# Making four expert-table blocks ready in empty buffers beside the query projection, and starting the gathers one step later, in a hybrid encoder layer on Trainium2

## The chip, the cores and the metric

The kernel runs on one core of a Trainium2 chip. The metric is device time in microseconds (us) of one execution; the time of a kernel is the median of its runs. Engines are named as the profile names them: PE is TensorE (the matmuls), PEld its weight load, DVE is VectorE, ACT is ScalarE, POOL is GpSimd, SP is SyncE, which here only issues DMA transfers.

## The reference

One layer: two parallel head groups, cross-attention into 256 memory tokens, and an expert-retrieval feed-forward part (PEER). The change touches the last one alone. `D_MODEL` is 1024, the sequence has 512 tokens, there are 8 retrieval heads, 128 x 128 = 16384 experts of one neuron each, and each head keeps 16 experts for a token.

```python
def _peer(h, w_query, sub_keys, expert_u, expert_v):
    B, S, D = h.shape
    q = (h @ w_query).reshape(B, S, PEER_HEADS, 2, PEER_KEY_DIM)
    sc = jnp.einsum('bshpk,hpnk->bshpn', q, sub_keys).astype(jnp.float32)
    v1, i1 = lax.top_k(sc[..., 0, :], PEER_TOPK)
    v2, i2 = lax.top_k(sc[..., 1, :], PEER_TOPK)
    n_cand = PEER_TOPK * PEER_TOPK
    cand = (v1[..., :, None] + v2[..., None, :]).reshape(B, S, PEER_HEADS, n_cand)
    cand_idx = (i1[..., :, None] * N_KEYS + i2[..., None, :]).reshape(B, S, PEER_HEADS, n_cand)
    top_s, pos = lax.top_k(cand, PEER_TOPK)
    idx = jnp.take_along_axis(cand_idx, pos, axis=-1)
    g = jax.nn.softmax(top_s, axis=-1).astype(h.dtype)
    ...
    def block(args):
        xt, it, gt = args
        u = expert_u[it]
        act = jax.nn.gelu(jnp.einsum('td,tkd->tk', xt, u))
        return jnp.einsum('tk,tkd->td', gt * act, expert_v[it])
```

## The kernel before, in words

Every fp32 matmul is made of three on fp32r halves (`mm3`, L109): a weight tile is split into a high half `wh` (a cast on ACT) and a low half `wl` (the rest).

The 512 tokens are four tiles of 128. For tile 0 the selected rows of both expert tables are gathered, one row per token and slot: 128 gathers from U and 128 from V, in order, by indirect DMA from POOL, each followed by one DVE instruction (`gather_step`, L1101). For tiles 1 to 3 (384 tokens) the kernel computes all 16384 experts densely: for each of 128 blocks e of 128 experts, `mm1(e)` multiplies U block e by the tokens (24 matmuls of 384 columns) and applies GeLU; the result lies in a buffer `act` until `weigh(e)` multiplies it by the gate weights, and `second` multiplies it by V block e. `mm1` runs `LAG` = 40 blocks ahead of `second`; the pool `acts` has 42 buffers of 128 x 384.

Stages, in the order of the program:

- Query projection (L853 to L905): for n = 0 to 15 a block `pq` of the query weight is multiplied (`proj`), the query is copied (`query`), scored against its keys (`key_scores`), and DVE takes the first 16 of each head half (`first_level`).
- Blocks ahead of the rows (L1033 to L1039): while `second_level(1)` selects the 16 experts of each head for token tile 1 on DVE, PE computes the first `U_MID` = 10 blocks of U. The generator `second_level` yields after each of its 15 steps.
- One-hot rows (L1041 to L1085): for tiles 1 to 3 the gate weights are scattered into a dense matrix `Wd` in DRAM: 32 groups of four tokens a tile, each with `hot` and `wei` on DVE and eight matmuls (L1063), an eviction on ACT, and a store for every four groups. Between groups parts of further `mm1` blocks are emitted at a `rate` that reaches block 37 at the end, and steps of `second_level` for the next tile.
- Main loop (L1204 to L1256), in an order written by hand: three more blocks, then 128 steps e, each with `mm1(e + 40)`, `weigh`, two steps of `second_level(0)` twice, gathers up to `due(e + 0.4)` and `due(e + 1)`, and `second`. `due` gives no gather before step `G_AT`, and spreads 215.6 of the 256 up to step 88 whatever `G_AT` is. For tile 0 the temporary tiles of `second_level` lie in the gather buffers (`Rooms`).

Outside the hand-ordered part a scheduler orders each engine's instructions by program order and readiness; each engine then runs them strictly in that order.

Weights come through `Weights`: `plan` lists all blocks in order of use, `get` hands out the next, `fill` loads and casts up to `DEPTH` = 2 ahead, `fill_low` makes the low halves. The pool `wp` has three buffers each of `w`, `wh` and `wl`. For most blocks U0 to U36 the low half is made by a DMA: ACT writes -w into `wl` (L144) and POOL issues a transfer that adds w minus the rounding (L145); blocks 11, 14, ..., 35 and 37 to 39 are split by DVE (L174). A raw buffer `w` is free again when its low half is done.

Of the kernel before, what the change touches and what calls it, by code (L numbers as in the profile page):

```python
# [10 lines left out]
F32 = mybir.dt.float32  # L11
F32R = mybir.dt.float32r
# [4 lines left out]
AF = mybir.ActivationFunctionType  # L17
# [12 lines left out]
ND = DT * 128  # L30
NE = 128
LAG = 40
U_MID = 10
SPARE = 3
WGB = 3
GPB = 4
# [11 lines left out]
OFF1 = 600  # L48
OFF2 = 10
LEVEL = 2, 3  # L50
G_AT = 3
L_MID = 2
WARM = 9
QAHEAD = 1
# [22 lines left out]
def layer(ctx, tc, a, out, upto=99, dbg=None):  # L77
    nc = tc.nc
    dbg = dbg or {}
    V, A, PE, SP, PL = nc.vector, nc.scalar, nc.tensor, nc.sync, nc.gpsimd  # L80

    def pool(stack, name, bufs=1, **kw):
        return stack.enter_context(tc.tile_pool(name=name, bufs=bufs, **kw))
# [9 lines left out]
    def bank(name="bk"):  # L93
        return psum.tile([128, 512], F32, name=name, tag="bk")
# [5 lines left out]
    def split(hi, lo, src):  # L100

        A.copy(hi, src)
        V.tensor_sub(lo, src, hi.bitcast(F32))
# [5 lines left out]
    def mm3(ps, terms, first=True, last=True):  # L109
        n = len(terms)  # L110
        for c, (lh, ll, rh, rl) in enumerate(terms):
            PE.matmul(ps, lh, rh, start=first and c == 0, stop=False)  # L112
            PE.matmul(ps, lh, rl, start=False, stop=False)  # L113
            PE.matmul(ps, ll, rh, start=False, stop=last and c == n - 1)  # L114

    class Weights:

        def __init__(self, plan):  # L120
            self.plan, self.raw, self.ready, self.at, self.low, self.used = plan, {}, {}, 0, 0, 0
            self.more = None

        def low_tile(self, key, shape):

# [1 line left out]
            return pool.tile(shape, F32R, name="wl")  # L127

        def fill(self, n, cuts=(slice(None),), between=None):
            while self.at < min(n, len(self.plan)):  # L130
                key = self.plan[self.at]
                self.at += 1
                src, shape, by_dma = source(*key)
                w = wp.tile(shape, F32, name="w")
                wh = wp.tile(shape, F32R, name="wh")
                for cs in cuts:
                    SP.dma_start(w[:, cs], src[:, cs])
                    A.copy(wh[:, cs], w[:, cs])  # L138
                    if between:
                        between.pop()()  # L140
                wl = None
                if by_dma:
                    wl = self.low_tile(key, shape)
                    A.activation(wl, w, AF.Copy, scale=-1.0)  # L144
                    PL.dma_start(wl, w, accum_op=OP.add)  # L145
                self.raw[key] = w, wh, wl, shape
# [17 lines left out]
            self.at = self.low = n  # L164

        def fill_low(self, n, cuts=(slice(None),)):
            while self.low < min(n, len(self.plan)):
                key = self.plan[self.low]
                self.low += 1
                w, wh, wl, shape = self.raw.pop(key)  # L170
                if wl is None:
                    wl = self.low_tile(key, shape)
                    for cs in cuts:
                        V.tensor_sub(wl[:, cs], w[:, cs], wh[:, cs].bitcast(F32))  # L174
                self.ready[key] = wh, wl

        def get(self, *key, ahead=DEPTH):
            assert self.plan[self.used] == key, (self.plan[self.used], key)
            self.used += 1
            self.fill(self.used + ahead)  # L180
            self.fill_low(self.used + min(1, ahead))
            return self.ready.pop(key)

    def source(kind, n):
        one = [128, NCH, 128]
        if kind == "v":
            return a["w_v"][:, 2 * n:2 * n + 2], [128, 2, 512], kind in BY_DMA
        if kind == "mv":
            return a["w_vm"][:, n], [128, D], kind in BY_DMA
        if kind == "U":  # L190
            return a["U"][n], [128, D], n < LAG - U_DMA and n not in U_V
        if kind == "V":
            return a["V"][n * 128:(n + 1) * 128], [128, D], False
        at = {"xl": ("w_in", 0), "gt": ("w_in", 4), "q": ("w_in", 8), "k": ("w_in", 12), "mk": ("w_km", 0),
              "wo": ("w_out", 0), "qm": ("w_qm", 0), "om": ("w_om", 0), "pq": ("w_pq", 0)}[kind]
        return a[at[0]][at[1] + n], one, kind in BY_DMA
# [14 lines left out]
    W = Weights(plan)  # L211

    def proj(key, ops, n=S, **kw):
        wh, wl = W.get(*key, **kw)
        ps = bank()
        mm3(ps[:, :n], [(wh[:, c], wl[:, c], h[:, :n], l[:, :n]) for c, (h, l) in enumerate(ops)])
        return ps
# [73 lines left out]
    views, at = {}, 0  # L291
# [523 lines left out]
    ap = pool(ctx, "acts", LAG + 2, side="right")  # L815
# [19 lines left out]
    def mm1_next():  # L835
        ahead[0] += 1
        return mm1_parts(ahead[0] - 1)

    top_pool = ExitStack()
    tp = pool(top_pool, "top")  # L840
# [12 lines left out]
    with tc.tile_pool(name="qp", bufs=1) as qp:  # L853
        QS, SC, KEY = {}, {}, {}

        def load_keys(n):
            if n < 16:
                KEY[n] = qp.tile([128, 128], F32, name="kr", bufs=4)
                SP.dma_start(KEY[n], a["keysT"][n])

        def query(n):
            ps = PQ.pop(n)
            QS[n] = qp.tile([128, S], F32, name="q", bufs=3)
            if n < NQ:
                V.tensor_mul(QS[n], ps, R3)
            else:
                A.copy(QS[n], ps)
            load_keys(n + 2)

        def key_scores(n):  # L870

            SC[n] = qp.tile([128, TT, 128], F32, name="sc", bufs=4)
            ps = bank()
            for t in range(TT):
                ts = slice(t * 128, (t + 1) * 128)
                PE.matmul(ps[:, ts], QS[n][:, ts], KEY[n], start=True, stop=True)  # L876
            A.copy(SC[n].rearrange("p t n -> p (t n)"), ps)

        def first_level(n):
            h, p = divmod(n, 2)  # L880
            v, x, sc = [y[:, h, p] for y in vals], [y[:, h, p] for y in idxs], SC[n]
            rest = [qp.tile([128, 128], F32, name="s2", bufs=4) for t in range(TT)]
            for t in range(TT):
                V.max(v[t][:, :8], sc[:, t])
            for t in range(TT):
                V.max_index(x[t][:, :8], v[t][:, :8], sc[:, t])
            for t in range(TT):
                V.match_replace(rest[t], v[t][:, :8], sc[:, t], LOW)
            for t in range(TT):
                V.max(v[t][:, 8:], rest[t])  # L890
            for t in range(TT):
                V.max_index(x[t][:, 8:], v[t][:, 8:], rest[t])

        load_keys(0)
        load_keys(1)
        query(0)
        for n in range(16):
            if NQ <= n + QAHEAD < 16:
                PQ[n + QAHEAD] = proj(("pq", n + QAHEAD), ho)
            if n + 1 < 16:  # L900
                query(n + 1)
            key_scores(n)
            if n:
                first_level(n - 1)
        first_level(15)  # L905


    Wd = dram.tile([128, 8 * DT, NE, 16], F32)
    HK = [128, 8, 16]
# [24 lines left out]
    def second_level(t, tp):  # L934
# [10 lines left out]
        top = tp.tile(HK, F32, name="tops")  # L945
        pos = tp.tile(HK, U32, name="pos")
        for h0 in range(0, 8, 4):
# [13 lines left out]
                V.max_index(pos[:, h, 8:], top[:, h, 8:], c2[:, h - h0])  # L961
            yield

        p7 = tp.tile(HK, U32, name="p7")
        p3 = tp.tile(HK, U32, name="p3")
        ov = tp.tile(HK, F32, name="ov")
# [14 lines left out]
        for p in range(2):  # L981
# [11 lines left out]
            V.tensor_add(dst.rearrange("p (h k) -> p k h", k=16), eq[:, 0], eq[:, 1])  # L993
            out.append(dst)
            yield

        ex = tp.tile(HK, F32, name="ex")
        su = sm.tile([128, 8], F32, name="su8")
        gF = tp.tile([128, 128], F32, name="gF", bufs=2)
        V.tensor_sub(ex, top, top[:, :, 0:1].to_broadcast(HK))  # L1000
        A.activation(ex, ex, AF.Exp)
        V.tensor_reduce(su, ex, axis=AX.X, op=OP.add)
        V.reciprocal(su, su)
        V.tensor_mul(gF.rearrange("p (h k) -> p h k", k=16), ex, su[:, :, None].to_broadcast(HK))
# [19 lines left out]
    def hurried(steps, offset):  # L1024
        while True:
            with tc.high_priority(offset=offset) if offset else ExitStack():
                if next(steps, 0) == 0:
                    return
            yield

    with (tc.tile_pool(name="wg", bufs=2) as wg, tc.tile_pool(name="st", bufs=2, side="right") as stages,
          tc.tile_pool(name="wx", bufs=1) as W.more):
        parts, owed = iter(()), 0.0  # L1033
        done = 0
        for k, _ in enumerate(hurried(second_level(1, tp), OFF1)):
            while ahead[0] < LAG and done < (k + 1) * U_MID / 15 and done < U_MID:
                done += 1
                for _ in mm1_next():
                    pass  # L1039
        rate = (LAG - SPARE - ahead[0]) * NCH / (DT * 32)  # L1040
        for tile_ in range(1, TT):  # L1041
            level = hurried(second_level(tile_ + 1, tp) if tile_ < DT else iter(()), OFF2)
            ij, gg = SEL.pop(tile_)
            for q in range(8):
                tb = (tile_ - 1) * 8 + q
                stage = stages.tile([128, NE, 16], F32, name="stage", tag="stage")
                for t4 in range(0, 16, 4):
# [22 lines left out]
                    while owed >= 1:  # L1070
                        owed -= 1
                        if next(parts, 0) == 0 and ahead[0] < LAG - SPARE:
                            parts = mm1_next()
# [79 lines left out]
    def due(e):  # L1153

        full = NE - LAG
        late = (256 - G_RATE * full) / (LAG - G_END)
        return math.ceil(G_RATE * max(min(e, full) - G_AT, 0) * full / (full - G_AT) + late * max(e - full, 0))

# [46 lines left out]
    order.enter_context(tc.manual_schedule())  # L1205

    level = second_level(0, Rooms(gp))

    def level_steps(n):
# [111 lines left out]
```

## Time and profile before

| | us |
|---|---|
| median of 3 runs (1628.90 to 1629.57) | 1629.24 |
| the profiled execution, its own time | 1627.87 |
| its span, from the first to the last instruction | 1626.1 |
| PE busy | 1592.0 |
| DVE busy | 1267.4 |
| ACT busy | 753.7 |
| POOL busy | 469.4 |

Times in the profile count from the start of the span. A matmul's record is longer than the distance to the next one, since matmuls are pipelined: the distance between starts is what a matmul costs. A record in brackets tells how long the engine stood idle before the instruction and what ended the wait.

### The profile page before, as it was taken

To read this page: it belongs to the slowest core of one execution; us is meant where nothing else is said; L and a number is where in the kernel's file an instruction comes from. 1 tells how busy PE (TensorE), PEld (TensorE's weight loads), DVE (VectorE), ACT (ScalarE), POOL (GpSimd) and SP (SyncE) were. 2 spreads that over 40 slices of the span, in tenths; PEclk is the share of its full clock that TensorE was granted. 3 is DMA by queue.
4 is the path that set the end of the run, shared out by engine and by line. 5 is a ranking of instruction groups with operands and counts; after the bars stand their busy time and mean duration, and the time that the engine had idled before them with its cause. 6 is when DMAs were issued, how large, how long until landed. Compare 5 with 4: busy or idle time off the path is not lost.

```text
span 1626.1 us, 23694 instructions
## 1 busy us (share of the span) xinstructions
PE 1592.0 (98%) x8512; PEld 1401.8 (86%) x8512; DVE 1267.4 (78%) x2525; ACT 753.7 (46%) x1194; POOL 469.4 (29%) x345
## 2 busy tenths in 40 slices
PE   9999999999997999999999999999999999999997
PEld 7788888888887888998999999999999999988886
DVE  7878885555979997887777777777777777788887
ACT  6568753456455676643333333333333333333334
POOL 0111000001111100004455454444444554453331
PEclk9999999999999999999999999999999999999999
DMA  7444452127777899977989889998898898999993
GB/s 257 123 136 146 126 164 96 56 74 222 168 174 174 257 308 269 300 234 276 316 300 320 307 301 320 312 318 308 291 332 313 298 317 309 307 328 335 319 329 145
DMA packets 156359, 405.83 MB, mean 250 GB/s; under 512 B 13793, under 2 KB 63073, under 8 KB 153169
## 3 DMA queue, kind: packets, MB, share of 16 engines
q1 hardware_dynamic: 110736, 242.36, 43.4%
q0 software_dynamic: 45504, 161.96, 32.5%
q8 instruction: 66, 1.08, 0.3%
q14 instruction: 53, 0.43, 0.1%
HBM read 348.69 MB, written 29.36 MB: 232 GB/s over the span
## 4 chain that ended last, share of the span: by engine, by line
PE 87%; DVE 4%; DMA 4%; ACT 2%; issue 2%; POOL 0%; DVEq 0%; SPq 0%; ACTq 0%; POOLq 0%
PE acc L1167 31%; PE bk L112 16%; PE bk L113 15%; PE bk L114 15%; PE bk L1063 2%; DMA w<-in_U 1%; DMA Wd<-stage 1%; PE om L113 1%; PE om L114 1%; PE om L112 1%; PE bk L876 1%; DVE hot L1054 1%; DVE wei L1058 1%; PE pv L112 1%; PE pv L113 1%
## 5 line engine op out<-in xcount | busy, mean ns | idle before, releaser
L138 ACT CAST wh<-w 128x1024 fp32r<-128x1024 f32 x330 | 347.3, 1053 | 339.6 <-PE acc L1167 200.9
L112 PE MATMUL bk<-hH,wh 128*128 128x384 f32 (+1 forms) x1128 | 394.5, 350 | 4.2 <-ACT wh L138 4.2
L114 PE MATMUL bk<-hH,wl 128*128 128x384 f32 (+1 forms) x1128 | 386.8, 343 | 7.9 <-DVE wl L174 3.0
L113 PE MATMUL bk<-hL,wh 128*128 128x384 f32 (+1 forms) x1128 | 385.4, 342 | 0.0
L174 DVE TENSOR_TENSOR wl<-w,wh 128x1024 fp32r<-128x1024 f32 x286 | 348.6, 1219 | 26.8 <-ACT wh L138 26.5
L1097 POOL DMA_INDIRECT g<-in_Un,gidx x128 | 206.0, 1609 | 242.6 <-DVE junk L1104 197.5
L1097 POOL DMA_INDIRECT g<-in_V,gidx x128 | 199.1, 1555 | 229.0 <-DVE gacc L1114 213.0
L1167 PE MATMUL acc<-wh,ph 128*128 128x512 f32 x768 | 238.6, 391 | 0.0
L1167 PE MATMUL acc<-wh,pl 128*128 128x512 f32 x768 | 238.1, 391 | 0.0
L1167 PE MATMUL acc<-wl,ph 128*128 128x512 f32 x768 | 238.1, 390 | 0.0
L114 PEld LDWEIGHTS bk<-hH,wl 128*128 128x128 f32 x1128 | 212.7, 189 | 13.8 <-DMA wl<-w 3.9
L112 PEld LDWEIGHTS bk<-hH,wh 128*128 128x128 f32 x1128 | 213.0, 189 | 11.8 <-ACT wh L138 4.8
L113 PEld LDWEIGHTS bk<-hL,wh 128*128 128x128 f32 x1128 | 213.0, 189 | 7.0
L1144 DVE TENSOR_TENSOR pl<-act,ph 128x384 fp32r<-128x384 f32 x128 | 71.1, 557 | 181.8 <-ACT ph L1141 181.8
L826 ACT ACTIVATE act<-bk 128x384 f32<-128x384 f32 x128 | 62.8, 493 | 282.6 <-PE bk L114 282.5
L145 POOL DMA_DIRECT2D wl<-w x44 | 37.8, 858 | 485.2 <-ACT wl L144 444.1
L1167 PEld LDWEIGHTS acc<-wl,ph 128*128 128x128 f32 x768 | 144.1, 188 | 31.6
L1167 PEld LDWEIGHTS acc<-wh,pl 128*128 128x128 f32 x768 | 144.1, 188 | 31.2
L1167 PEld LDWEIGHTS acc<-wh,ph 128*128 128x128 f32 x768 | 142.9, 188 | 24.2
L1114 DVE SCALAR_TENSOR_TENSOR gacc<-g,gu,gacc 128x1024 f32<-128x1024 f32 x127 | 162.5, 1279 | 0.7
L1104 DVE SCALAR_TENSOR_TENSOR junk<-g,htok 128x1024 bf16<-128x1024 f32 x128 | 156.0, 1219 | 6.0 <-DMA g<-in_Un,gidx 5.1
L112 PE MATMUL bk<-oh,wh 128*128 128x512 f32 x280 | 111.8, 400 | 0.1
(338 smaller groups left out, 2140.8 us busy)
## 6 DMA issues: line engine op xcount, KB each, us to landing
w<-in_U SPq DMA_DIRECT2D x128, 512.0 KB, 5.2
w<-in_V SPq DMA_DIRECT2D x128, 512.0 KB, 5.9
Wd<-stage SPq DMA_DIRECT2D x24, 1024.0 KB, 6.6
wt<-Wd SPq DMA_DIRECT2D x90, 256.0 KB, 6.9
wl<-w POOLq DMA_DIRECT2D x44, 512.0 KB, 6.1
w<-in_w_pq SPq DMA_DIRECT2D x16, 512.0 KB, 4.8
w<-in_w_in SPq DMA_DIRECT2D x14, 512.0 KB, 3.5
x<-in_xT SPq DMA_DIRECT2D x16, 256.0 KB, 4.6
```

The costliest lines, as they stand in the source:

```text
L112: PE.matmul(ps, lh, rh, start=first and c == 0, stop=False)
L113: PE.matmul(ps, lh, rl, start=False, stop=False)
L114: PE.matmul(ps, ll, rh, start=False, stop=last and c == n - 1)
L138: A.copy(wh[:, cs], w[:, cs])
L145: PL.dma_start(wl, w, accum_op=OP.add)
L174: V.tensor_sub(wl[:, cs], w[:, cs], wh[:, cs].bitcast(F32))
L826: A.activation(ACT[e], ps[:, :ND], AF.Gelu_apprx_tanh)
L1097: PL.indirect_dma_start(out=g, out_offset=None, in_=a[table], in_offset=bass.IndirectOffsetOnAxis(ap=gidx[:, k:k + 1], axis=0))
L1104: V.scalar_tensor_tensor(junk, g, 1.0, htok, op0=OP.mult, op1=OP.mult, accum_out=gu[:, st:st + 1])
L1114: V.scalar_tensor_tensor(gacc, g, gu[:, k:k + 1], gacc, op0=OP.mult, op1=OP.add)
L1144: V.tensor_sub(PS[e][1], ACT.pop(e), PS[e][0].bitcast(F32))
L1167: PE.matmul(acc[t, hf], lhs[:, ts], rhs[:, hf * 512:(hf + 1) * 512], start=e == 0 and part == 0, stop=e == NE - 1 and part == 2)
```

## The change

Four things change.

- `U_EARLY`: after steps 7, 9, 11 and 13 of the query projection, `Weights.early` makes one of the blocks U0 to U3 ready. It loads the block in thirds (384, 384 and 256 columns) into buffers of the pool `acts`, and splits each third with a cast on ACT and a subtraction on DVE: nine buffers a block, 36 of the 42. `Thirds` lets the matmuls index the three pieces as one tile.
- `reach` lets `fill` and `fill_low` go as many blocks further as there are early ones among those not yet used, so that the three `wp` buffers go to U4, U5, U6.
- `U_MID` is 8 instead of 10: two blocks more are emitted among the one-hot rows.
- In `second_level` the exponential `ex` stands right after the second selection; before, it stood after the index steps. `G_AT` is 4 instead of 3.

```diff
-U_MID = 10
+U_MID = 8
+U_EARLY = 7, 9, 11, 13
...
-G_AT = 3
+G_AT = 4
...
+    class Thirds:
+        def __init__(self, parts):
+            self.parts = parts
+        def __getitem__(self, at):
+            k, c = divmod(at[1].start, ND)
+            return self.parts[k][:, c:c + at[1].stop - at[1].start]
...
-            self.more = None
+            self.more, self.lead = None, set()
+
+        def reach(self, n, at):
+            return min(n + sum(key in self.lead for key in self.plan[self.used:at]), len(self.plan))
+
+        def early(self, key, pool):
+            src, shape, _ = source(*key)
+            thirds = [slice(k, min(k + ND, shape[1])) for k in range(0, shape[1], ND)]
+            parts = []
+            for cs in thirds:
+                n = cs.stop - cs.start
+                w, wh, wl = [pool.tile([128, ND], dt, name=k, tag="act")[:, :n]
+                             for k, dt in (("ew", F32), ("eh", F32R), ("el", F32R))]
+                SP.dma_start(w, src[:, cs])
+                split(wh, wl, w)
+                parts.append((wh, wl))
+            self.ready[key] = [Thirds([p[k] for p in parts]) for k in range(2)]
+            self.lead.add(key)
...
         def fill(self, n, cuts=(slice(None),), between=None):
-            while self.at < min(n, len(self.plan)):
+            while self.at < self.reach(n, self.at):
                 key = self.plan[self.at]
                 self.at += 1
+                if key in self.ready:
+                    continue
...
         def fill_low(self, n, cuts=(slice(None),)):
-            while self.low < min(n, len(self.plan)):
+            while self.low < self.reach(n, self.low):
                 key = self.plan[self.low]
                 self.low += 1
+                if key in self.ready:
+                    continue
...
         def get(self, *key, ahead=DEPTH):
             self.used += 1
+            self.lead.discard(key)
...
             if n:
                 first_level(n - 1)
+            if n in U_EARLY:
+                W.early(("U", U_EARLY.index(n)), ap)
         first_level(15)
...
                 V.max_index(pos[:, h, 8:], top[:, h, 8:], c2[:, h - h0])
             yield
 
+        ex = tp.tile(HK, F32, name="ex")
+        V.tensor_sub(ex, top, top[:, :, 0:1].to_broadcast(HK))
+        A.activation(ex, ex, AF.Exp)
+
         p7 = tp.tile(HK, U32, name="p7")
...
             yield
-
-        ex = tp.tile(HK, F32, name="ex")
         su = sm.tile([128, 8], F32, name="su8")
         gF = tp.tile([128, 128], F32, name="gF", bufs=2)
-        V.tensor_sub(ex, top, top[:, :, 0:1].to_broadcast(HK))
-        A.activation(ex, ex, AF.Exp)
         V.tensor_reduce(su, ex, axis=AX.X, op=OP.add)
```

## Rows read from the trace of the kernel before

**Rows 1.** From the page, busy time and share of the span of PE and its weight load, with the number of instructions.

```profile
PE 1592.0 (98%) x8512; PEld 1401.8 (86%) x8512; DVE 1267.4 (78%) x2525; ACT 753.7 (46%) x1194; POOL 469.4 (29%) x345
```

**Rows 2.** Busy time by stretches. Columns: the stretch in us, its length, the busy time of each engine in it (with the number of instructions), the granted clock of PE, the share of the DMA engines, GB/s.

```profile
400.00:450.00 50.00, 50.00 (x254) 42.56 (x253) 42.84 (x290) 26.05 (x37) 6.32 (x9) 1.00 0.77 185
...
481.00:535.00 54.00, 44.98 (x245) 43.05 (x243) 51.44 (x266) 28.85 (x39) 7.71 (x9) 0.97 0.74 178
535.00:577.00 42.00, 39.95 (x340) 35.47 (x339) 39.07 (x109) 32.73 (x53) 4.29 (x5) 1.00 0.90 268
...
604.00:650.00 46.00, 45.27 (x388) 40.92 (x388) 37.62 (x55) 30.07 (x50) 4.29 (x5) 1.00 0.90 275
650.00:705.00 55.00, 55.00 (x471) 50.06 (x469) 46.92 (x74) 33.16 (x54) 3.62 (x5) 1.00 0.88 294
...
760.00:1590.00 830.00, 830.00 (x4107) 744.07 (x4107) 644.48 (x812) 292.43 (x404) 394.99 (x249) 1.00 0.91 314
```

**Rows 3.** PE's instructions in order of time, from the first table block to the one-hot rows. Columns: start in us, length, engine, line, operation, tiles and shapes, count, idle time before it and what ended it.

```profile
480.88 0.42 PE L112 MATMUL bk<-hH,wh 128*128 128x384 f32 x1
...
504.18 0.44 PE L114 MATMUL bk<-hH,wl 128*128 128x384 f32 x1 [1.34 <-DMA wl<-w]
...
510.31 0.44 PE L112 MATMUL bk<-hH,wh 128*128 128x384 f32 x1 [1.69 <-ACT wh L138]
...
512.78 0.66 PE L114 MATMUL bk<-hH,wl 128*128 128x384 f32 x1 [1.86 <-DVE tops L951]
...
518.76 0.33 PE L114 MATMUL bk<-hH,wl 128*128 128x384 f32 x1
...
519.28 0.33 PE L114 MATMUL bk<-hH,wl 128*128 128x384 f32 x1
...
524.69 0.44 PE L112 MATMUL bk<-hH,wh 128*128 128x384 f32 x1 [2.47 <-ACT wh L138]
...
528.53 0.44 PE L114 MATMUL bk<-hH,wl 128*128 128x384 f32 x1 [1.65 <-DMA wl<-w]
```

**Rows 4.** The instructions that write PSUM banks from 478 to 545 us, grouped by line; shortest, median and longest in ns, start of the first and of the last.

```profile
L1063 PE MATMUL bk<-wei,hot x48: 218/218/238, 535.1 to 544.6; 128*128 128x128 f16 x48
```

**Rows 5.** The chain of work that ended last, from 470 to 580 us, in order of time: start, length, what. "issue" is time in which the engine waited for nothing that the profile shows.

```profile
494.25 3.97 DMA w<-in_U
...
499.74 8.36 issue
508.11 4.54 DMA wl<-w
512.71 5.96 DMA w<-in_U
```

**Rows 6.** Instructions of ACT and of POOL in order of time, same columns as rows 3.

```profile
503.95 0.78 ACT L984 CAST kn<-idx 128x128 f16<-128x128 uint32 x1 [3.65 <-DVE idx L892]
...
506.75 1.07 ACT L144 ACTIVATE wl<-w 128x1024 fp32r<-128x1024 f32 x1 [1.17 <-DVE idx L892]
...
481.65 0.86 POOL L145 DMA_DIRECT2D wl<-w  x1 [5.49 <-ACT wl L144]
```

**Rows 7.** Steps 2 to 4 of the main loop: PE's instructions, then DVE's, same columns.

```profile
743.29 0.45 PE L114 MATMUL bk<-hH,wl 128*128 128x384 f32 x1 [0.75 <-DVE wl L174]
...
754.09 0.45 PE L114 MATMUL bk<-hH,wl 128*128 128x384 f32 x1 [2.25 <-DVE wl L174]
...
755.07 0.51 PE L113 MATMUL bk<-hL,wh 128*128 128x384 f32 x1
...
758.26 0.45 PE L114 MATMUL bk<-hH,wl 128*128 128x384 f32 x1
...
740.65 0.29 DVE L1002 TENSOR_REDUCE su<-g 128x8 f32<-128x128 f32 x1 [2.00 <-ACT g L1001]
...
748.73 1.23 DVE L1104 SCALAR_TENSOR_TENSOR junk<-g,htok 128x1024 bf16<-128x1024 f32 x1 [3.42 <-DMA g<-in_Un,gidx]
```

**Rows 8.** DVE's instructions in order of time: the end of the selection for tile 1, for tile 2, and the wait after it.

```profile
508.63 0.37 DVE L993 TENSOR_TENSOR sel<-eq 128x128 f32<-128x128 f16 x1
...
533.45 0.38 DVE L993 TENSOR_TENSOR sel<-eq 128x128 f32<-128x128 f16 x1
...
535.76 0.69 DVE L1054 TENSOR_TENSOR hot<-io,ij 128x1024 f16<-128x1024 f16 x1 [1.59 <-PE bk L1063]
```

**Rows 9.** Waits of PE over the whole span: who waited for whom, us in total, times, the longest.

```profile
PE bk L1063 <- DVE wei L1058: 2.7, 5, 0.7
```

**Rows 10.** Beside the query projection: issues of SP's queue, then instructions of ACT; the last line is a cast of 128 x 384 from the main loop.

```profile
378.90 2.18 SPq L859 DMA_DIRECT2D kr<-in_keysT  x4
...
399.79 1.07 ACT L809 COPY xt<-bk 128x512 f32<-128x512 f32 x2 [2.78 <-DMA x3d<-xt]
...
433.95 1.04 ACT L138 CAST wh<-w 128x1024 fp32r<-128x1024 f32 x1 [3.37 <-issue]
...
717.72 0.50 ACT L1141 CAST ph<-act 128x384 fp32r<-128x384 f32 x1
```

**Rows 11.** From the page: a group of instructions (busy us in total, mean ns of one | idle time before), and two of the DMA issues (KB each, median us from issue to landing).

```profile
L1144 DVE TENSOR_TENSOR pl<-act,ph 128x384 fp32r<-128x384 f32 x128 | 71.1, 557 | 181.8 <-ACT ph L1141 181.8
...
w<-in_U SPq DMA_DIRECT2D x128, 512.0 KB, 5.2
...
x<-in_xT SPq DMA_DIRECT2D x16, 256.0 KB, 4.6
```

## Prediction

> **What bounds the kernel now.** I read the page first. TensorE (PE) is busy 98% of the span [rows 1], so only the stretches in which PE stands still or runs slowly can be won. The list of busy time by stretches comes second: PE has no loss from 400 to 450 us nor from 760 to 1590, and loses 9 of the 54 us from 481 to 535 and 2 of 42 after that [rows 2]. For these places, and for the start of the main loop, I then read PE's instructions in order of time with the idle time before each, the chain of waits, and the same stretch of ScalarE (ACT), VectorE (DVE) and GpSimd (POOL).
>
> First place: the ten table blocks ahead of the one-hot rows. Their first matmul starts at 480.9 [rows 3] and the first one-hot matmul at 535.1 [rows 4]: 54.2 us. Three matmuls start every 0.52 us (518.76 to 519.28), so a block of 24 takes 4.16 us and ten take 41.6; 12.6 us are lost. Five waits make 9.0 of them (1.34 + 1.69 + 1.86 + 2.47 + 1.65) [rows 3]; the rest is slower matmuls and short gaps. The chain says why: a raw block is loaded (3.97 us), the next issue of POOL comes 8.36 us later, the low half is accumulated by DMA (4.54), and only then is the raw buffer loaded again (5.96) [rows 5]. With three buffers this chain is slower than PE. The 8.36 us are ACT standing in order behind index casts (`kn`), the first of which waits 3.65 us for DVE [rows 6].
>
> Second place: steps 2 and 3 of the main loop. At step 2 DVE waits 2.00 us for the exponential of token tile 0 with the table load before it, and PE waits 0.75 us for a low half queued behind it. At step 3 DVE waits 3.42 us for the first gather and again for the second; the low half that PE needs stands behind them, and PE waits 2.25 us. From 755.07 to 758.26 ten matmuls then take 3.19 us instead of 10 x 0.173 = 1.74 [rows 7]: the clock was at its lower level.
>
> **Part A: four blocks made ready early, eight ahead of the rows.** U0 to U3 no longer need the three buffers; their halves lie in `act` tiles before PE reaches them. By `reach`, the buffers that now hold U0 to U2 take U4 to U6 instead. The last of these three is sent to its accumulation at 481.65 [rows 6], so all three are in hand long before PE gets to them, and PE can run U0 to U6 without a wait, to 480.9 + 7 x 4.16 = 510.0. U7 needs the cast buffer that U4 frees at 501.7. If ACT takes it at once, two casts of 1.07, an issue of 0.86 [rows 6] and a transfer of 4.54 to 5.96 [rows 5] end at 509.2 to 510.7: no wait. If ACT stands behind `kn` as now (506.75 + 1.07, then the accumulation from 508.11 to 512.65), U7 waits some 2 us. The one-hot rows need the selection of tile 1, which DVE ended at 509.0 (508.63 + 0.37) [rows 8] while PE was held up until 535; transposes, three small casts and the first one-hot pair put the first row at about 513 to 514, while U7 runs. So of 12.6 us lost I keep 2: **gain 10.6**. Bounds: 12.6 if nothing waits; 5.6 if the chain behind U7 is as bad as now and 7 us stay.
>
> **Part B: the rows with two more blocks among them.** The two blocks are moved, 8.3 us of the same matmuls, at 29 x 8 / 96 = 2.42 parts a row group instead of 2.25: no change in PE's sum. What changes is DVE's lead. At 533.45 DVE had already ended the selection of tile 2, and at 535.76 it stood waiting for PE [rows 8]; the selection of tile 3 then filled it, 39.07 of the 42 us to 577, against 37.62 of 46 and 46.92 of 55 after 604 [rows 2]. If the rows start about 18 us earlier, most of tile 2's selection falls among them. PE now waits for one-hot weights 2.7 us in all [rows 9]. Below: no extra wait, because the instruction order can put the selections off into the 16 us that DVE has free after 604 (8.4 + 8.1). Above: 11 us, about what PE has gained by then, on a DVE that puts nothing off. Nearest to the stretch to 577, where DVE was nearly as full and PE lost 2 us: I take **a loss of 2.5**.
>
> **Part C: the exponential moved up and the gathers one step later.** In the part ordered by hand `ex` now runs in the eighth step of the generator, at step 0 of the loop. Its subtraction and table load are paid there, on ACT between casts that have idle time before them, and DVE finds it done. `G_AT = 4` lets DVE reach the first gather one step of 8.3 us later, and its index is ready about 2 us sooner; a gather that landed at 748.7 is awaited after about 751, the second likewise. Both waits of PE and the slow stretch go: 0.75 + 2.25 + (3.19 - 1.74) = **4.45 gained**. The gathers' rate rises from 2.45 x 88/85 = 2.54 to 2.45 x 88/84 = 2.57 a step and meets the old one at step 88; DVE has room for it (busy 644 of 830 us there, and PE shows no wait [rows 2]). Bounds: 5 with short gaps counted, 2.2 if a later gather catches PE at step 4 instead.
>
> **Part D: the price beside the query projection.** Twelve loads, twelve casts and twelve subtractions are added: ACT at most 12 x 0.50 = 6.0 us [rows 10], DVE at most 12 x 0.557 = 6.7 [rows 11], in place of four times two casts of 1.07 on ACT and four accumulating transfers later. ACT has 3.37 us idle ahead of a block's cast [rows 10]; the DMA engines are busy 0.77 there [rows 2], so 2 MB more fit. What can hurt is order. SP issued four key loads together at 378.90, long before the last of them stands in the program, so loads with an empty buffer are sent early; a cast placed behind such a load blocks ACT until it lands, as the stores of `x3d` blocked it for 2.78 us at 399.79 [rows 10], where PE lost nothing. Below 0, above 8 us (two late loads of about 4 us each, the 256 KB load's 4.6 [rows 11] being the nearest row, with no slack to cover them); nearest to the case at 399.79: **0.5 lost**.
>
> The thirds go against a rule of the Trainium skill, page "DMA: Bandwidth & Descriptors", section "Rules for kernel authors": use 1 MiB or more per DMA. By linear estimate from that page's measured sizes (64 KB 0.95 us, 1 MB 6.15) a block in thirds takes 4.6 us of the engines instead of 3.4, some 5 us for four blocks; the sum would stay as it is while the share is below 1. The rows agree in direction (256 KB takes 4.6 us, 512 KB 5.2 [rows 11]).
>
> **Sum.** 10.6 - 2.5 + 4.45 - 0.5 = 12.05. The profiled execution took 1627.87 us (span 1626.1 and 1.8 around it); it becomes 1615.8. The median of the runs, 1629.24, lies 1.4 above the profiled one, so 1617.2; I say **1617**.
>
> **Rivals.**
> 1. *DVE becomes the bound among the rows.* For it: DVE is full from 535 to 577 even with its lead. Against: it has 16 us free after 604, and it waits for PE at 535.76. Part B then costs 8 to 11: total gain 3.5 to 6.5, time 1622.7 to 1625.7; say 1624.
> 2. *The supply stays short.* U4 to U6 come in time, but the chain of loads, casts and accumulations is as slow as ever, and PE meets it at U7 and among the first rows. For it: the 8.36 us are ACT's order, which the change does not touch. Against: among rows PE asks for a block less often than every 4.2 us. The change then does not do what it says; 7 of the 12.6 us stay: gain about 7, time 1622.
> 3. *Slower: early loads and casts hold up the query projection.* PE has no idle time there, so each microsecond by which a query weight is late counts in full. Every early block puts three casts in ACT's order; if each holds ACT until PE loses 4 us, that is 16 us, as much as parts A to C bring (12.55) with room to spare; from 3.1 us a block on the change costs time. Four blocks at 4 us: 16 - 12.55 = 3.5 slower, 1632.7. Against: 3.4 us of ACT's slack per query block.
> 4. *Nothing to measure*: the same mechanism at 2.4 to 3.9 us a block, 1626 to 1632.5.
>
> **Chances.** Forecast (1611 to 1621) 0.60; rival 1 0.16; rival 2 0.11; rival 4 0.07; rival 3 0.06. A measurement here tells 0.2%, 3.3 us, from no change: faster (below 1626.0) holds the forecast, rival 2 and nearly all of rival 1, 0.86; same 0.08; slower 0.06. The range: the best case is 12.6 + 2.7 + 5 = 20.3 gained, 1609; up to 1627 it takes in rivals 1 and 2 and leaves out rival 3 and most of 4: **1610 to 1627**.
>
> **What would show it.** A: in the changed profile the blocks follow each other at 4.16 us from about 481 to 510, the first one-hot matmul starts at 514 to 519, and no stretch near 513 runs at the lower clock. B: PE's wait for one-hot weights stays under 6 us. C: no wait of PE at steps 2 and 3 and no DVE wait for a gather. D: PE busy in full from 397 to 481. The prediction is wrong if PE waits in the query projection behind casts of the early tiles, if the first one-hot row does not come at least 15 us sooner, or if the stage of the rows takes more than 10 us longer than now (8.3 are the two blocks).

## The result and the profile after

| | before | after |
|---|---|---|
| median of five runs beside each other, us | 1629.40 (1628.90 to 1630.36) | 1621.45 (1618.49 to 1622.42) |
| median of five more runs of after, with 12 of before | 1628.41 | 1623.27 (1621.56 to 1624.34) |
| profiled execution, its span | 1627.87, 1626.1 | 1618.49, 1616.7 |

The ratio is 0.9948 (95%: 0.9933 to 0.9963) in the first comparison and 0.9966 (0.9952 to 0.9979) in the second: faster by 5 to 8 us where 12.05 were forecast. The profiled execution of after is the fastest of its ten runs (median 1622.0), so its trace flatters the change; a second trace (the run `after_again` below) was taken of one of the slower (1623.27). Of the runs below, each trace is of one execution too: that of sel_once is its fastest, those of hold_level, hold_c2 and dve_free are their slowest.

The page of after, busy time, to be held against [rows 1]:

```profile
PE 1588.9 (98%) x8512; PEld 1400.9 (87%) x8512; DVE 1270.4 (79%) x2537; ACT 752.6 (47%) x1200; POOL 468.8 (29%) x342
```

Busy time by stretches of after (columns as in [rows 2]):

```profile
400.00:450.00 50.00, 50.00 (x255) 42.53 (x254) 42.31 (x276) 27.93 (x42) 6.24 (x8) 1.00 0.85 211
...
480.00:486.00 6.00, 3.81 (x17) 3.77 (x17) 5.09 (x35) 3.56 (x5) 1.41 (x2) 0.72 1.03 190
487.00:518.00 31.00, 31.00 (x182) 30.97 (x181) 31.00 (x189) 15.60 (x23) 2.57 (x3) 1.00 0.44 102
521.00:530.00 9.00, 8.68 (x75) 8.03 (x75) 9.00 (x17) 8.40 (x12) 0.86 (x1) 1.00 0.74 214
590.00:602.00 12.00, 9.26 (x81) 8.41 (x81) 12.00 (x20) 7.16 (x12) 0.86 (x1) 1.00 0.92 307
...
740.00:760.00 20.00, 20.00 (x103) 18.16 (x102) 12.09 (x18) 7.45 (x11) 7.78 (x6) 1.00 1.01 376
```

The blocks ahead of the rows run without a gap (487 to 518: 31.00 of 31.00, where before five waits stood [rows 3]), and so does the start of the main loop (740 to 760), where PE and the gathers waited [rows 7]. The losses now stand elsewhere: at 480 to 486, at the first one-hot row and at 590 to 602. PE's three long waits of after from 400 us on, its instructions in order of time:

```profile
482.23 1.68 PE L911 MATMUL bk<-kr,q 128*128 128x128 f32 x8 [2.19 <-ACT q L902]
...
521.32 0.62 PE L1100 MATMUL bk<-wei,hot 128*128 128x128 f16 x8 [2.68 <-DVE wei L1095]
...
592.81 0.40 PE L1100 MATMUL bk<-wei,hot 128*128 128x128 f16 x4 [2.74 <-DVE wei L1095]
```

The first is in the query projection, the second is the first one-hot row (at 535.1 before [rows 4]), the third is among the rows, where PE's longest wait for weights was 0.7 us [rows 9].

Start times from the traces, made into lengths in us, divide the gain. "Query" runs from the first key score to the first table block, "blocks and rows" from there to the last one-hot row, "loop" from the first accumulation to that of its step 4; the parts left out differ from those of before by up to 1.2 us.

| trace | query | blocks and rows | loop | median of runs |
|---|---|---|---|---|
| before | 85.9 | 222.1 | 38.3 | 1629.4; 1627.45 to 1628.41 later |
| after | 88.0 | 214.7 | 33.2 | 1622.0 (ten runs) |
| after_again | 89.1 | 219.2 | 33.2 | the same kernel |
| c_only | 85.9 | 221.9 | 33.2 | 1623.4 |
| no_c | 88.5 | 217.8 | 37.0 | 1626.0 |
| mid8_only | 85.9 | 222.0 | 39.6 | 1629.4 (one run) |
| no_double | 86.9 | 220.5 | 33.2 | 1622.8 |
| mid9 | 88.6 | 218.1 | 33.2 | 1623.1 |
| early_mid10 | 89.4 | 218.8 | 33.2 | 1624.0 |
| hold_level | 90.2 | 218.4 | 33.2 | 1621.7 |
| hold_c2 | 90.4 | 216.7 | 33.2 | 1621.1 |
| sel_once | 88.2 | 211.7 | 33.2 | 1615.0 |
| no_double_c2 | 85.9 | 218.5 | 33.2 | 1620.2 |
| dve_free | 87.2 | 224.1 | 33.2 | 1622.9 |

### The profile page after: what moved, and what is told of

Read it like the earlier page. It is cut to its first block, busy times and chain, and to the rows that moved or that the text cites. A ratio compares the mean times of both kernels' runs of the same rounds, so it can differ in the third digit from the quotient of the medians.

```text
span 1616.7 us, 23709 instructions
## 1 busy us (share of the span) xinstructions
PE 1588.9 (98%) x8512; PEld 1400.9 (87%) x8512; DVE 1270.4 (79%) x2537; ACT 752.6 (47%) x1200; POOL 468.8 (29%) x342
## 4 chain that ended last, share of the span: by engine, by line
PE 89%; DVE 7%; ACT 2%; DMA 1%; issue 1%; SPq 0%; DVEq 0%; ACTq 0%
PE acc L1204 32%; PE bk L113 16%; PE bk L114 16%; PE bk L115 16%; PE bk L1100 2%; PE pv L113 1%; PE pv L115 1%; PE pv L114 1%; PE om L113 1%; PE om L115 1%; PE om L114 1%; DVE hot L1091 1%; DVE wei L1095 1%; PE bk L911 1%; PE po L593 1%
## 5 line engine op out<-in xcount | busy, mean ns | idle before, releaser
L113 PE MATMUL bk<-hH,wh 128*128 128x384 f32 (+1 forms) x1096 | 382.3, 349 | 0.0
L115 PE MATMUL bk<-hH,wl 128*128 128x384 f32 (+1 forms) x1096 | 374.1, 341 | 0.0
L114 PE MATMUL bk<-hL,wh 128*128 128x384 f32 (+1 forms) x1096 | 373.4, 341 | 0.0
L114 PEld LDWEIGHTS bk<-hL,wh 128*128 128x128 f32 x1096 | 206.1, 188 | 7.0
L113 PEld LDWEIGHTS bk<-hH,wh 128*128 128x128 f32 x1096 | 205.9, 188 | 7.0
L115 PEld LDWEIGHTS bk<-hH,wl 128*128 128x128 f32 x1096 | 205.7, 188 | 4.1
```

## The experiments

**Part C alone, and all but part C.** Edits: `G_AT` 3 to 4 and the moved `ex` on the kernel before; the reverse on the kernel after.

> The kernel before with part C alone: the exponential made ahead of the one-hot rows, and the gathers one loop step later. My theory (each part acts in its own place, and the loop of the changed kernel is shorter by what part C gave): the same saving as between the two profiles, where the time from the first accumulation of the loop to that of its step 4 fell from 38.3 to 33.2 us, so 5.1 us faster than before, 1624.3; no PE wait at steps 2 and 3 and no stretch at the lower clock near 755. Rival (part C works only because the rows come 14 us earlier and DVE therefore reaches the loop with a lead): the wait for the gather comes back at step 4, gain 0 to 2.5 us, 1627 to 1629.

> The changed kernel with the exponential in its old place and the gathers at step 3 (parts A, B and D alone). My theory: the waits of steps 2 and 3 come back in full, 5.1 us slower than the changed kernel, 1626.5, and 2.9 us faster than before. Rival (an earlier row stage gives DVE a lead that hides the gathers by itself, so that part C is not needed): 0 to 2 us slower than the changed kernel, 1621.5 to 1623.5.

Measured: c_only 1623.39 against 1627.84, ratio 0.9968 (0.9956 to 0.9981); no_c 1626.03, ratio 0.9988 (0.9974 to 1.0002). PE in c_only is full where [rows 7] shows waits:

```profile
740.00:762.00 22.00, 22.00 (x113) 20.08 (x113) 15.97 (x23) 7.18 (x10) 11.48 (x8) 1.00 0.95 351
```

The slow stretch behind the second wait, in the kernel before:

```profile
755.00:758.50 3.50, 3.50 (x13) 3.50 (x12) 3.50 (x7) 0.00 (x0) 1.69 (x1) 0.51 0.96 313
```

In no_c both waits are back, PE's instructions in order of time:

```profile
741.70 0.45 PE L115 MATMUL bk<-hH,wl 128*128 128x384 f32 x1 [0.78 <-DVE wl L208]
...
752.75 0.44 PE L115 MATMUL bk<-hH,wl 128*128 128x384 f32 x1 [2.49 <-DVE wl L208]
```

Part C works by itself: c_only has 5.1 us less in the loop, and its median falls by 4.45. Taken away it costs 3.8 in the trace (37.0 against 33.2) and some 4 in the medians; in no_c the clock did not fall after the second wait, which is the missing 1.3. Part C is thus well over half of the whole gain, and A, B and D together bring about 2 (no_c: 1.8, with an interval that takes in no gain at all).

**Only U_MID = 8, nothing early.** Edit: `U_MID = 8` in the kernel before.

> The kernel before with eight instead of ten table blocks ahead of the one-hot rows, nothing made ready early. One theory (the supply of blocks is the shortage, and rows give it time): the seven blocks after the third lose 12.6 us, so five lose about 9; the two moved blocks no longer wait, gain 2 to 4 us, 1625.5 to 1627.5, and the first row at about 524 us. Rival (the selection of tile 1 on DVE, ended at 509, and what stands behind it set the first row; rows then wait for their weights): what the blocks give, the rows give back, 1629 with more than 5 us of PE waits for one-hot weights.

Measured: 1629.41, a single run. The first row comes at 518.60, sooner than in the changed kernel, but the time from the first block to the last row is that of before (222.0 and 222.1). PE's waits:

```profile
513.09 0.44 PE L114 MATMUL bk<-hH,wl 128*128 128x384 f32 x1 [3.02 <-DMA wl<-w]
...
597.23 0.64 PE L1063 MATMUL bk<-wei,hot 128*128 128x128 f16 x8 [2.92 <-DVE wei L1058]
```

In this one trace an early first row is worth nothing by itself; the rows give it back. With no block made early, it stands 37.3 us behind the first block, where the two traces of after have 37.8 and 38.2: that the first row comes sooner is thus not shown to come from the early blocks.

**The second loading of U3.** Edit:

```diff
-U_EARLY = 7, 9, 11, 13
+U_EARLY = 7, 9, 11, 12
```

The page of after lists one load of U more than the 128 - 4 = 124 that are left:

```profile
w<-in_U SPq DMA_DIRECT2D x125, 512.0 KB, 5.4
```

The page of no_double:

```profile
w<-in_U SPq DMA_DIRECT2D x124, 512.0 KB, 5.0
```

By the code, the buffers of the `wp` pool are filled at step 13 of the query projection before `early` makes U3 known there: U3 is loaded, cast and accumulated a second time, and nobody reads it. So the three buffers take U3, U4 and U5, not U4 to U6 as the description of the change and the prediction say.

> The changed kernel with the fourth early block one query block sooner, which ends the second, unread loading and casting of that block in the ordinary buffers. My theory (the last query block waits 2.2 us for its query copy because that copy stands in ACT's order behind the high cast of the second loading, and PE's clock falls to the lower level after that wait): both go, first one-hot row 3 to 4 us sooner, 1617.5. Rival (the copy is late for another reason, or the wait moves to the first row, where PE already waits 2.7 us for DVE): 0 to 1 us, 1620.5 to 1621.5.

Measured: 1622.81, ratio 0.9960 (0.9946 to 0.9974). ACT of after, in order of time: two waits behind loads of early thirds, then the query copy that PE waits for, which stands behind a cast that waits for its load.

```profile
410.78 0.52 ACT L103 CAST eh<-ew 128x384 fp32r<-128x384 f32 x1 [5.01 <-DMA ew<-in_U]
...
430.66 0.41 ACT L103 CAST eh<-ew 128x256 fp32r<-128x256 f32 x1 [5.80 <-DMA ew<-in_U]
...
480.65 1.04 ACT L170 CAST wh<-w 128x1024 fp32r<-128x1024 f32 x1 [1.24 <-DMA w<-in_U]
481.60 0.58 ACT L902 COPY q<-bk 128x512 f32<-128x512 f32 x1
```

By the order of the loads and casts this is not the cast of the second U3, as the expectation has it, but that of U6, the fourth table block to go through the pool. Its load found no raw buffer until the accumulation of the second U3's low half had freed one. The chain of after_again, where the wait is 3.41 us, runs through these steps:

```profile
472.35 5.77 DMA wl<-w
...
478.18 3.16 DMA w<-in_U
...
482.37 0.58 ACT q L902
```

The load of U6 is issued at 477.43 in after and at 471.99 in no_double.

PE's waits in no_double:

```profile
481.52 1.16 PE L911 MATMUL bk<-kr,q 128*128 128x128 f32 x8 [0.55 <-ACT q L902]
...
514.51 0.44 PE L115 MATMUL bk<-hH,wl 128*128 128x384 f32 x1 [1.85 <-DMA wl<-w]
```

The wait for the query copy falls to 0.55; in the eight traces with the second loading (sel_once included) it is 1.95 to 3.96, in the three without it 0.55, 0.55 and 1.71. The 1.71 (dve_free) has another cause: ACT stood 3.20 us behind the load of an early third, until 476.65, and was late at all that followed. What is won comes back: the last block's low half is 1.85 us late, the first row waits 3.3 us, and the clock falls for 6.8 us there.

**The same kernel again.**

> The changed kernel again, nothing edited. The runs of the kernel before and of the others so far differ among themselves by up to 6 us. My theory: the places at which PE waits do not move, and what varies is how many stretches of 3.4 us at the lower clock follow those waits, each about 1.7 us; so 1619 to 1623 us, the first one-hot row at 521.3 and the last at 698.3 where no such stretch falls among the rows, at 700 where one does. Rival (DVE's work or the transfers themselves vary): the waits themselves are of other lengths or in other places.

Measured: 1623.27 (1621.56 to 1624.34). PE's three waits stand in the same places:

```profile
483.00 1.16 PE L911 MATMUL bk<-kr,q 128*128 128x128 f32 x8 [3.41 <-ACT q L902]
...
522.10 0.76 PE L1100 MATMUL bk<-wei,hot 128*128 128x128 f16 x8 [3.28 <-DVE wei L1095]
...
594.80 1.04 PE L1100 MATMUL bk<-wei,hot 128*128 128x128 f16 x8 [2.74 <-DVE wei L1095]
```

Busy time by stretches of after_again:

```profile
480.00:486.00 6.00, 3.00 (x20) 3.00 (x21) 5.05 (x35) 3.61 (x6) 2.07 (x3) 1.00 1.06 217
...
521.00:530.00 9.00, 7.90 (x57) 7.28 (x57) 8.95 (x16) 7.23 (x10) 0.86 (x1) 0.81 0.74 214
590.00:602.00 12.00, 9.26 (x58) 8.46 (x56) 10.80 (x17) 5.47 (x10) 0.86 (x1) 0.72 0.76 242
```

The clock column is the difference: behind the waits at 522 and 594 it fell here (0.81 and 0.72; in after 1.00 both), behind that at 482 it fell in after (0.72; here 1.00). PE loses 0.19 x 9 + 0.28 x 12 = 5.1 us of work among the rows; 4.4 of the 4.8 us between the two spans lie in blocks and rows. The waits themselves vary too (2.2 and 3.4 us), so the rival holds in part.

**More blocks ahead of the rows.** Edits: `U_MID = 9` and `U_MID = 10` in the kernel after.

> The changed kernel with nine blocks ahead of the rows instead of eight. My theory (PE stands 2.8 us at the first row for DVE, with a block ready): the ninth block fills that wait, first row at 522.5, the wait gone, 2 to 3 us faster than the changed kernel run beside it. Rival (the rows are bound by DVE, and a block taken from among them is missed there): the wait goes to the rows, 0 us; or the ninth block's halves are late as the eighth's were in the run without the second loading (1.9 us), 0 to 1 us.

> The changed kernel with ten blocks ahead of the rows, as the kernel before has, so that only the early making (parts A and D) and part C are left of it. My theory: the last two blocks may wait some 2 us for halves, the first row comes at 526 to 528 after PE without the 2.8 us wait, DVE has 5 us more of a lead, and the waits for weights among the rows (6.3 us in the changed kernel) fall under 2: 2 to 5 us faster than the changed kernel. Rival (blocks are needed among the rows to cover DVE): waits of 3 us or more for weights stay, no gain.

Measured: 1623.10, ratio 0.9966 (0.9952 to 0.9979), and 1624.00, ratio 0.9972 (0.9962 to 0.9983): no better than after. The first row in mid9, then in early_mid10:

```profile
529.21 1.01 PE L1100 MATMUL bk<-wei,hot 128*128 128x128 f16 x8 [5.29 <-DVE wei L1095]
```

```profile
536.05 1.01 PE L1100 MATMUL bk<-wei,hot 128*128 128x128 f16 x8 [6.81 <-DVE wei L1095]
```

Both expectations failed: with more blocks ahead PE waits longer at the first row, not shorter, because DVE's order then has still more of the selections in front of its one-hot tensors. The waits among the rows do shrink, and with nine or ten the length of blocks and rows (218.1 and 218.8) lies between the two traces of after. The run early_mid10 also has all that c_only has, and the early blocks besides: 1624.00 against 1623.39. With ten blocks ahead of the rows, making four of them early brings no time.

**DVE's order at the first row.** DVE of after, in order of time (the end of tile 1's selection, the end of what then runs of tile 2's selection, the first one-hot tensor):

```profile
511.05 0.38 DVE L1034 TENSOR_TENSOR sel<-eq 128x128 f32<-128x128 f16 x1
...
519.05 0.22 DVE L1014 TENSOR_SCALAR t<-p 128x128 f32<-128x128 uint32 x1
519.19 0.68 DVE L1091 TENSOR_TENSOR hot<-io,ij 128x1024 f16<-128x1024 f16 x1
```

From 511.25 to 519.19 DVE is at tile 2's selection. ACT has the indices ready at 515.4, so the last 3.8 of these 7.9 us hold the one-hot tensors up. Edits, in `second_level` behind `gg` for t = 1, first of hold_level, then of hold_c2:

```diff
+        if t == 1:
+            V.tensor_copy(cand[:, 0, 0:2], gg[:, 0, 1, 0:2])
```

```diff
+        if t == 1:
+            V.tensor_copy(c2[:, 0, 0:2], gg[:, 0, 1, 0:2])
```

> The changed kernel with one small copy added on DVE, which lets the candidates of tile 2 start only when tile 1's reduced weights are made; DVE's order then has tile 1's one-hot tensors ahead of tile 2's selection (8 us of work that now stands in front of them). My theory (DVE's order sets the first row): first row about 517.5 to 518.5, no wait there, and what follows the stage keeps at least half of it: 1.5 to 3 us faster than the changed kernel run beside it. Rival (DVE is the bound among the rows, so an order cannot help): the 2.7 us come back as waits for one-hot weights in the 40 us after, 0 us.

> The changed kernel with one small copy on DVE that holds tile 2's selection after its first maxima and indices, until tile 1's reduced weights are made: some 3.4 us of it stay ahead of the first one-hot tensors (the hold of before left DVE idle for 5.4 us there), 5 us come after them. My theory (in the run with the longer hold, the first row's gain was paid back because DVE, which bounds the rows, stood idle): DVE idle under 1.5 us, first row at 517 to 519, and 2 to 3 us faster than the changed kernel run beside it (1622.7 over its ten runs), 1620. Rival (DVE's sum decides, whatever its order): the waits come back among the rows, 0 to 1 us.

Measured: hold_level 1621.65 against 1623.27 of after beside it, ratio to before 0.9951 (0.9937 to 0.9964); hold_c2 1621.08, ratio 0.9956 (0.9943 to 0.9968). The wait at the first row is gone in both. In hold_level DVE waits instead, and PE's waits among the rows are many and small:

```profile
517.40 0.69 DVE L1093 TENSOR_TENSOR hot<-io,ij 128x1024 f16<-128x1024 f16 x1 [5.39 <-ACT ij L1056]
```

```profile
PE bk L1102 <- DVE wei L1097: 5.6, 9, 1.2
```

The chain of hold_level from 518 to 562 us is DVE's but for 0.4 us of issue, for instance:

```profile
548.43 1.20 DVE hot L1093 x2
549.63 0.60 DVE wei L1097
550.23 0.60 DVE eq L1032
550.84 0.60 DVE wei L1097
```

So the order set the first row, as I held, but most of it was paid back, as the rival held. Leaving 3.4 us of the selection ahead (hold_c2) brought blocks and rows to 216.7; the medians of the two cannot be told apart, and neither lies clear of the ten runs of after (1618.5 to 1624.3). Their median is 1622.0, not 1622.7 as the expectation of hold_c2 has it, so hold_c2 is 0.9 us lower: what the rival gave it.

**DVE's work taken away.** Edits, `sel_once` then `dve_free` (on the kernel of no_double_c2, the last experiment below):

```diff
-            level = hurried(second_level(tile_ + 1, tp) if tile_ < DT else iter(()), OFF2)
-            ij, gg = SEL.pop(tile_)
+            level = iter(())
+            ij, gg = SEL[1]
```

```diff
-U_V = *range(11, LAG - U_DMA, 3), *range(LAG - U_DMA, LAG)
+U_V = *range(26, LAG - U_DMA, 3), *range(LAG - U_DMA, LAG)
```

> The changed kernel with the selections of tiles 2 and 3 left out: the one-hot rows of all three tiles use the indices and weights of tile 1, so what the later tiles add up is not the kernel's. About 2 x 20 us of DVE's work among the rows are gone, PE's work is the same. My theory (DVE bounds the stage of the rows, by its sum and by what stands in front of the first row): first row at 517 to 518, no wait of more than 1 us for weights after it and so no stretch at the lower clock among the rows; 182.5 us from the first block to the last row at most 175, 6 to 9 us faster than the changed kernel beside it, 1614. Rival (the waits among the rows come from the blocks' supply, or from PE's own order): waits of 2 us and more stay, gain at most 3 us.

Measured: 1614.99, ratio 0.9925 (0.9908 to 0.9941), 7 us below the ten runs of after. The kernel before ran faster beside it too (1627.45), and by the ratios to it the gain over after is 4 to 7 us. Blocks and rows take 211.7 us (214.7 and 219.2 in the two traces of after; the 182.5 of the expectation is not this length): the first row stands 34.7 us behind the first block (37.8 and 38.2), and the rows take 176.9 (177.0 and 181.0). The edit takes the selections' work away from ACT and PE as well, so it does not tell DVE's share from theirs. One wait of PE over 0.5 us is left among the rows, so this part of the theory failed, and it runs back over three engines. PE, then DVE, then ACT of sel_once:

```profile
551.64 0.64 PE L1100 MATMUL bk<-wei,hot 128*128 128x128 f16 x8 [3.42 <-DVE wei L1095]
```

```profile
549.03 1.22 DVE L208 TENSOR_TENSOR wl<-w,wh 128x1024 fp32r<-128x1024 f32 x1 [6.26 <-ACT wh L170]
```

```profile
546.98 1.09 ACT L1102 ACTIVATE stage<-bk 128x512 f32<-128x512 f32 x2 [5.24 <-DMA Wd<-stage]
```

ACT stands at an eviction whose buffer `stage` the store has not yet freed, the cast of the next block behind it, DVE behind that cast. The chain shows what stands ahead of the store:

```profile
528.65 8.70 DMA wl<-w
...
537.41 0.33 SPq L169
...
537.79 9.09 DMA Wd<-stage
```

The last eviction into that buffer had ended at 531.8. The store was issued 6 us later, because in SP's order a load stood in front of it, and that load waited for a raw buffer until the accumulation had ended. So the selections cost the rows some 4 to 7 us, and behind them comes the store of `Wd`, held up by SP's order.

> The run before (hold, no second loading) with five low halves among the rows (blocks 11, 14, 17, 20, 23) taken off DVE: ACT casts them and DMA accumulates them, as it does for their neighbours. My theory (DVE bounds the rows until about 620): five subtractions of 1.21 us and an idle of 2.2 us in front of one of them are gone, the 5.8 us of PE waits for weights fall under 3, the last row comes 3 to 6 us sooner after the first block than in that run (218.5), 1616 to 1618. Rival (ACT and the DMA engines, whose share is 0.95 from 535 to 580, are as full as DVE): PE waits for low halves instead, 2 us or more, 1620 to 1623.

Measured: 1622.90, ratio 0.9965 (0.9953 to 0.9977), 2.7 us slower than no_double_c2 by the medians. My theory fell: five subtractions less on DVE (6.1 us) did not help. DVE's two longest waits behind ACT among the rows are 5.20 and 6.30 us, against 2.57 and 2.21 in no_double_c2, and the longer goes back to the store again. DVE, then ACT of dve_free:

```profile
631.59 1.23 DVE L208 TENSOR_TENSOR wl<-w,wh 128x1024 fp32r<-128x1024 f32 x1 [6.30 <-ACT wh L170]
```

```profile
630.03 0.60 ACT L1104 ACTIVATE stage<-bk 128x512 f32<-128x512 f32 x1 [4.03 <-DMA Wd<-stage]
```

The rival's place (PE waiting for low halves) was wrong too; this wait came through ACT and the store. Part of the 224.1 us in the table is the clock, which fell three times in this trace between 515 and 639 us. A third `stage` buffer would test the store, and an issue of the store ahead of the loads would test SP's order; neither was tried.

**Both mends together.** Edits: those of no_double and hold_c2.

> The hold of the run before together with the fourth early block one query block sooner (no second loading). My theory: 2 to 4 us at the last query block and 2 to 3 us at the first row, less the 2 us that PE waited for the eighth block's low half in the run with the earlier block alone: 1618 to 1619.5. Rival (what is won upstream meets the same DVE later): 1621.

Measured: 1620.23, ratio 0.9953 (0.9940 to 0.9965), the lowest median of a complete kernel, 1.8 below the ten runs of after; that is within what the runs vary. The query projection is back at 85.9 in this trace (86.9 and 87.2 in the two others without the second loading), and blocks and rows stay at 218.5.

## Why the prediction came out as it did

The time, 1621.45, lies in the range 1610 to 1627, and faster was right. The time lies just outside the 1611 to 1621 that the forecast itself claimed: the sum of 12.05 was too large by 4 us in the first comparison, by 7 in the second. Two of the prediction's own signs of being wrong came. The first one-hot row is 13.8 us sooner (13.0 in after_again), where it asked for 15. The rows take 177.0 us in after and 181.0 in after_again against 167.9 before, 9.1 and 13.1 more, where it allowed 10.

- **Part C**, forecast 4.45: 5.1 in the trace, 4.45 in the median of c_only. Its working held, place by place: both waits and the slow stretch went, and at these steps DVE waits for no gather. Of the surplus of 0.6, the clock explains 0.3: at 0.51 over 3.5 us it cost 1.7, where the sum had 1.45. The rest stays open, and it is not short gaps: PE's records of before show no idle time in this part of the loop but the two waits.
- **Part A**, forecast 10.6: 8.1 in the trace of after (54.2 us less two blocks of 4.16 became 37.8), 7.7 in after_again. The blocks ran without a wait, as the step said, apart from 0.7 us at the last in after_again. Of the 4.5 us that are lost in after, where 2 were allowed, 2.7 are the wait at the first row and some 1.3 the lower clock at the start of the blocks (0.50 from 483.6 to 486.1). The step that failed is the one from the selection of tile 1 to the first row, "at about 513 to 514": its transposes and casts were sized rightly (done at 515.4, 4 us after the selection), but the step let the one-hot pair follow at once, where DVE had tile 2's selection first. How much of these 8 us the early blocks bring is not shown (mid8_only reaches its first row as soon without them).
- **Part B**, forecast -2.5: -0.8 in after, where the clock did not fall, and -4.8 in after_again, where it fell twice (5.1). A and B together, 8.1 by forecast, are 7.3 and 2.9 in the two traces. The mechanism that rival 1 named, DVE full among the rows, is at work: PE's waits for weights rose from 2.7 [rows 9] to 6.3 us (the prediction had named 6 as the sign), sel_once, without two selections, is 4 to 7 us faster, and the gain of the medians, 5 to 8, straddles the upper end of that rival's 3.5 to 6.5. I had trusted the 16 us that DVE has free after 604 [rows 2]; the selections stand before them.
- **Part D**, forecast -0.5: the query projection grew by 2.1 and 3.1 us. The loads of the thirds raised the share of the DMA engines from 0.77 [rows 2] to 0.85, below 1 as the sum supposed. The danger that I named did come, ACT standing 5.0 and 5.8 us behind early loads, and cost PE nothing in after, as I took it (in dve_free it did). Most of the loss came from a load that I had not seen, U3's second, which kept a raw buffer from U6; the step that failed here is "the buffers that now hold U0 to U2 take U4 to U6".
- **The clock** stood in the sum only where it was lost before. The three new waits sum to 7.6 us in after and 9.4 in after_again, and the lower clock behind them cost 1.7 and 5.1 us more; that had no term.

Of rival 2 a small part was seen: the last block's low half is 1.9 us late once the second U3 is gone. Rival 3 did not come.

## What to carry to other kernels

When a stage is to start sooner, follow its first instruction through the fixed order of every engine that feeds it: time won on PE is only worth what the next in-order queue lets through, and here it was DVE's order, then an eviction behind a store, and the store behind a load. Count the loads on the page after a change of prefetch: one too many showed the double work at once. Price a new wait of the matmul engine with what the clock may take behind it, and take two traces of the same kernel before a sum is made from one.

## What was not expected of the hardware

The same kernel with the same wait of 2.74 us at the same place ran on at a granted clock of 1.00 in one trace and at 0.72 over the 12 us around it in another (590 to 602, above). Over the ten runs of no_c the mean granted clock goes from 0.998 in the fastest (1623.0 us) to 0.994 in the slowest (1630.8): 0.004 of the span is 6.5 us. The clock is thus part of what runs of one kernel differ by here, but not all: at 0.995 the times go from 1625.3 to 1629.9 us. What decides whether it falls stays open.
